# A gated MLP layer on one core: all its input products in one stage with seven-for-eight column pairs, the token mixing moved behind it

## The chip, the cores and the metric

The kernel runs on one core of a Trainium2 chip. What is measured is its time on the device in microseconds (us). The engines are named as in the profile: PE is TensorE's matmul and PEld its weight load, DVE is VectorE, ACT is ScalarE, POOL is GpSimd, and SP starts the weight loads. A line number is one of the kernel's file.

## The reference

One step of a two-layer encoder on two prompt blocks and one sample block of 128 tokens, model width 2048, all in fp32. Layer 0 is attention (two kinds of heads), and the change does not touch it. Layer 1 is a gated MLP of width 4096:

```
u, v, z = rmsnorm(h) @ w_in1                  # three parts, 4096 columns each
vn      = layernorm(v)                        # over all 4096 columns of a token
mixed   = w_sp[g] @ vn + b_sp                 # tokens of a block, causal, per group of 256 columns
h       = h + (u * mixed * silu(z)) @ w_out1
y       = rmsnorm(h)
```

The normalised v of the sample block is an output too. The norm over all columns means that no mixing can start before the whole of v is there.

## The kernel before, in words

Three token blocks (NT = 3, 384 tokens) stand against 16 k-blocks of 128 (KT) and column blocks of 512; u, v and z have eight column blocks each. Every fp32 product is made of three matmuls on halves: each operand is split into a high part and the rest, and hi x hi, hi x lo and lo x hi are added in one PSUM bank (`products`, L94; matmuls L100, L101, L102). A weight unit is one 128x512 block, 256 KB: SP loads it into `raw` (5 buffers), ACT makes `whi` (L84) and DVE `wlo` (L86), 4 buffers each (`wunit`). A dense column block (`dense_nat`, L108) takes three of the four PSUM banks named "d", one for each token block, and runs over the 16 units; hooks given as `between` put other work between its units, with that work's instructions placed behind the splits of the units before. The order on each engine is fixed when the program is built, by a scheduler; each engine takes its own queue in that order.

Before `seven`, layer 1 makes v blocks 0 and 1 densely. Then two column pairs follow, (2,3) and (4,5), in `seven`: for the two prompt blocks and two column blocks, a 2x2 scheme with seven products in place of eight, and four more for the sample block: 11 block products of 24 matmuls where 12 were. It has three phases, `singles`, `chain` and `pair`, each in four steps u over k. In the last two, the operands are sums of weight blocks, made by DVE from loads of 512 KB (`load2`, five buffers named sraw; sums L943) before they are split (shi L90, slo L91; three buffers each); the matmuls are at L930 to L932, into four banks named "a". The blocks v6 and v7 are made the ordinary way between those steps: three units ahead of each step of `chain`, one ahead of each step of `pair`. All v goes to DRAM (`vd`), 768 KB for a block.

Then a loop runs over c = 0..7: z block c, evicted with silu into `gate` (L1139); u block c, multiplied in (L1147); v block c + 1 loaded and normalised meanwhile (L1066, L1067); the mixing of block c, 12 matmuls (L1166 to L1168), the product with the gate (L1170), and the turn: a transposition on DVE (L132) and 16 DMAs on POOL's queue (L135) into gTt, four hi copies on ACT (L1177) and four lo copies on DVE (L1178). After c = 2, 4 and 6 `out1` multiplies 8 more k-blocks by w_out1; the last 8 come behind the loop, the final four of them in a hand-placed stage with the final norm.

Of the kernel before, what the change touches and what calls it, by code (L numbers as in the profile page):

```python
# [15 lines left out]
P = 128  # L16
# [21 lines left out]
def tile_hybrid_step(  # L38
# [828 lines left out]
    with ExitStack() as l1:  # L867
# [6 lines left out]
        vd = [dram.tile([P, NT, 512], F32, name=nm("vd")) for _ in range(8)]  # L874

        with ExitStack() as lv:
            vp = lv.enter_context(tc.tile_pool(name="l1v", bufs=1, reuse_waits="tile"))

            def evict_v(c, o):
                v = slot(F32).rearrange("p (t c) -> p t c", t=NT)  # L880
                for tb in range(NT):
                    S.activation(v[:, tb, :], o[tb], AF.Copy)  # L882
                done_v(c, v)

            def done_v(c, v):
# [28 lines left out]
            def load2(u, half, c):  # L914

                raw = wide()
                nc.sync.dma_start(raw, w_in1[4 * u * P:4 * (u + 1) * P, CW + c * 512:CW + c * 512 + 512].rearrange("(j h p) c -> h p j c", h=2, p=P)[half])
                return raw
# [15 lines left out]
            def seven(c):  # L934

                v0, v1 = (slot(F32).rearrange("p (t c) -> p t c", t=NT) for _ in range(2))
# [8 lines left out]
                def singles(u):  # L945
                    if u == 0:
                        banks("1", "p", "2", "q")
                    b11, b21 = split2(load2(u, 0, c)), split2(load2(u, 1, c))
# [6 lines left out]
                def close_singles():  # L955
                    S.activation(v1[:, 0], m["1"], AF.Copy)
                    S.activation(v1[:, 2], m["p"], AF.Copy)
                    add(v0[:, 0], m["2"], v1[:, 0])
                    add(v0[:, 2], m["q"], v1[:, 2])

                def chain(u):
                    if u == 0:
                        banks("5", "r", "6", "4")
                    b11, b12, b22, b21 = load2(u, 0, c), load2(u, 0, c + 1), load2(u, 1, c + 1), load2(u, 1, c)
# [17 lines left out]
                def pair(u):  # L982
                    if u == 0:
                        banks("3", "s", "7")
                    b22, b12 = load2(u, 1, c + 1), load2(u, 0, c + 1)
# [8 lines left out]
                def close_pair():  # L994
# [4 lines left out]
                    done_v(c, v0)  # L999
                    done_v(c + 1, v1)  # L1000
# [3 lines left out]
            def eight(c):  # L1004
# [3 lines left out]
                def one(k):  # L1008
                    if k == 0:
                        o.extend(dbank() for _ in range(NT))  # L1010
                    ws = [wunit(w_in1[k * P:(k + 1) * P, CW + c * 512:CW + c * 512 + 512], 1, 512)]
                    return lambda: products(o, hh_, hl_, ws, k, range(NT), 0, KT - 1)

                return one, lambda: evict_v(c, o)
# [17 lines left out]
            for c, c8 in ((2, 6), (4, 7)):  # L1032
                (b1, e1), (b2, e2), (b3, e3) = seven(c)
                one, close = eight(c8)
                steps = [(b1, u) for u in range(4)] + [(e1, None)]
                for u in range(4):
                    steps += [(one, 3 * u + i) for i in range(3)] + [(b2, u)]
                steps += [(e2, None)]
                for u in range(4):
                    steps += [(one, 12 + u), (b3, u)]  # L1040
                run(steps + [(e3, None)])
                close()
        for tb in range(NT):
            V.bn_aggr(out=mvr[:, tb, :], in_=stats[:, tb, :, :])
        G.tensor_tensor(out=rsv, in0=mvr[:, :, 1], in1=rstd, op=ALU.mult)
        G.tensor_tensor(out=rsv, in0=rsv, in1=rstd, op=ALU.mult)
        G.tensor_scalar(out=rsv, in0=rsv, scalar1=LN_EPS, scalar2=None, op0=ALU.add)
        G.tensor_tensor(out=rsv, in0=rsv, in1=ex, op=ALU.pow)
        G.tensor_tensor(out=rsv, in0=rsv, in1=rstd, op=ALU.mult)
# [7 lines left out]
        def normalise(c):  # L1057

            cs = slice(c * 512, (c + 1) * 512)
            lg = lp.tile([P, NT * 4, P], F32, tag="gTt", bufs=1, name=nm("lg")).rearrange("p x q -> p (x q)")[:, :1024].rearrange("p (a c) -> p a c", a=2)  # L1060
# [9 lines left out]
        load_v(0)  # L1070
        for _ in normalise(0):
            pass
# [52 lines left out]
        def split_values(c):  # L1125

            vh = lp.tile([P, NT * 4, P], F32R, tag="trn", bufs=1, name=nm("vh")).rearrange("p (t x) q -> p t (x q)", t=NT)
# [5 lines left out]
        vhl = split_values(0)  # L1133
        for c in range(8):
            wTs = [spatial_weights(2 * c + i) for i in range(2)]
            o = dense_nat(w_in1, 0, 2 * CW + c * 512, hh_, hl_)
            gate = lp.tile([P, NT, 512], F32, tag="gate", bufs=1, name=nm("gate"))
            for tb in range(NT):
                S.activation(gate[:, tb, :], o[tb], AF.Silu, scale=rstd[:, tb:tb + 1])  # L1139
            ahead = iter(())  # L1140
            if c < 7:
                load_v(c + 1)
# [3 lines left out]
            for tb in range(NT):  # L1146
                V.scalar_tensor_tensor(out=gate[:, tb, :], in0=o[tb], scalar=rstd[:, tb:tb + 1], in1=gate[:, tb, :], op0=ALU.mult, op1=ALU.mult)  # L1147
            if c == 7:

                for j in range(2):  # L1150
# [8 lines left out]
            for i in range(2):  # L1159
                cs = slice(i * 256, i * 256 + 256)  # L1160
                (wh, wl), (vh, vl) = wTs[i], vhl

                for j, tbs in ((0, slice(0, 2)), (1, slice(2, 3))):
                    n = tbs.stop - tbs.start
# [132 lines left out]
```

## Time and profile before

| | |
|---|---|
| median of 3 runs | 1782.47 us (1780.71 to 1785.07) |
| the profiled execution | 1781.91 us |
| its span | 1779.8 us |
| mean granted TensorE clock | 0.998 |
| PE, DVE, ACT, POOL busy | 1767.2, 1030.3, 740.9, 399.0 us |
| DMA, read and written in HBM | 291.64 MB, 35.71 MB |

The profile is that of one execution. The page gives the busy time of each engine; windows give it for a stretch of time; groups of instructions give count, busy time, mean ns of one, and the idle time ahead of them with what ended it; waits list who waited for whom; a timeline lists instructions with start, length and, in brackets, the idle time before. Matmuls overlap in TensorE's pipeline, so what one costs is the distance of starts, not its own length.

### The profile page before, as it was taken

How to read it: one execution, taken by the hardware profiler on the slowest of the kernel's cores; microseconds unless marked ns; L12 is line 12 of the kernel's file. 1: busy time of each engine (PE TensorE's matmuls, PEld its weight loads, DVE VectorE, ACT ScalarE, POOL GpSimd, SP SyncE). 2: the span in 40 equal slices, each digit the busy share in tenths (PEclk: the TensorE clock that was granted, in tenths of full speed). 3: DMA queues.
4: the chain of work that ended last, by engine and by line, in shares of the span. 5: the costliest groups of instructions: out<-in, count | busy, mean ns of one | idle time of the engine just before them, and what ended most of it. 6: DMA issues, size and time to landing. Idle time of an engine off the chain costs nothing. (4 is left out here: it accounts for less than half of the span.)

```text
span 1779.8 us, 24513 instructions
## 1 busy us (share of the span) xinstructions
PE 1767.2 (99%) x8515; PEld 1464.4 (82%) x8515; DVE 1030.3 (58%) x1674; ACT 740.9 (42%) x1289; POOL 399.0 (22%) x605
## 2 busy tenths in 40 slices
PE   9999999999999999999999999999999999999998
PEld 8978888888888888888887888888888888888887
DVE  6337565457448354677778556555456545454366
ACT  5435354346337244444443433433333333433344
POOL 6525534223311210100112231321021200220020
PEclk9999999999999999999999999999999999999999
DMA  8788989878868977677885655655455643564453
GB/s 228 198 208 202 274 215 229 236 171 217 234 187 213 258 183 165 183 257 229 262 246 185 220 147 158 180 151 154 130 155 156 167 143 125 160 154 135 155 148 119
DMA packets 195244, 335.31 MB, mean 188 GB/s; under 512 B 23768, under 2 KB 62224, under 8 KB 195120
## 3 DMA queue, kind: packets, MB, share of 16 engines
q1 hardware_dynamic: 135888, 242.15, 46.4%
q0 software_dynamic: 28400, 75.47, 17.3%
q10 hardware_dynamic: 30832, 16.13, 3.1%
q8 instruction: 66, 1.08, 0.3%
q14 instruction: 58, 0.48, 0.1%
HBM read 291.64 MB, written 35.71 MB: 184 GB/s over the span
## 5 line engine op out<-in xcount | busy, mean ns | idle before, releaser
L101 PE MATMUL d<-wlo,slot 128*128 128x512 f32 x2157 | 837.8, 389 | 0.0
L102 PE MATMUL d<-whi,slot 128*128 128x512 f32 x2157 | 837.6, 389 | 0.0
L86 DVE TENSOR_TENSOR wlo<-raw,whi 128x512 fp32r<-128x512 f32 x706 | 483.9, 696 | 579.8 <-ACT whi L84 575.9
L84 ACT ACTIVATE whi<-raw 128x512 fp32r<-128x512 f32 x706 | 443.8, 631 | 793.0 <-PE d L102 732.1
L100 PE MATMUL d<-whi,slot 128*128 128x512 f32 x2157 | 761.4, 390 | 1.5 <-ACT whi L84 1.5
L100 PEld LDWEIGHTS d<-whi,slot 128*128 128x128 f32 x2157 | 404.5, 188 | 89.8 <-ACT whi L84 3.1
L101 PEld LDWEIGHTS d<-wlo,slot 128*128 128x128 f32 x2157 | 405.0, 188 | 84.0 <-DVE wlo L86 1.0
L102 PEld LDWEIGHTS d<-whi,slot 128*128 128x128 f32 x2157 | 404.9, 188 | 84.2 <-DVE slot L278 0.3
L135 POOL DMA_DIRECT2D gTt<-trn x128 | 78.1, 617 | 149.2 <-DVE trn L132 110.9
L90 ACT ACTIVATE shi<-sraw 128x1024 fp32r<-128x1024 f32 x56 | 59.4, 1062 | 73.3 <-PE a L932 61.9
L91 DVE TENSOR_TENSOR slo<-sraw,shi 128x1024 fp32r<-128x1024 f32 x56 | 67.7, 1220 | 12.8 <-ACT shi L90 12.7
L464 POOL DMA_DIRECT2D slot<-d x48 | 44.0, 924 | 132.2 <-DMA d<-slot 54.1
L943 DVE TENSOR_TENSOR sraw<-sraw,sraw 128x1024 f32<-128x1024 f32 x32 | 39.1, 1223 | 31.7 <-DMA sraw<-in_w_in_dram 29.8
L1114 POOL DMA_DIRECT2D wr<-in_w_sp_dram x64 | 35.0, 553 | 83.7 <-DVE wT L1118 76.1
L563 POOL DMA_DIRECT2D slot<-wd x32 | 27.1, 855 | 93.9 <-DMA wd<-pr 32.8
L1068 POOL DMA_DIRECT2D out_dram<-v x8 | 4.5, 558 | 183.8 <-DVE v L1067 183.8
L931 PE MATMUL a<-slo,slot 128*128 128x512 f32 x112 | 43.7, 390 | 0.0
L932 PE MATMUL a<-shi,slot 128*128 128x512 f32 x112 | 43.6, 389 | 0.0
L888 POOL DMA_DIRECT2D vd<-slot x8 | 4.4, 551 | 168.6 <-ACT slot L882 162.8
L930 PE MATMUL a<-shi,slot 128*128 128x512 f32 x112 | 41.9, 389 | 0.0
L1107 DVE TENSOR_TENSOR slot<-d,slot 128x512 f32<-128x512 f32 x48 | 31.7, 686 | 11.6 <-PE d L102 11.5
L524 POOL DMA_DIRECT2D kcache<-in_cache_sb_k_dram x32 | 24.9, 786 | 34.0 <-DVE KT L694 34.0
(303 smaller groups left out, 1579.4 us busy)
## 6 DMA issues: line engine op xcount, KB each, us to landing
raw<-in_w_in_dram SPq DMA_DIRECT2D x576, 256.0 KB, 3.3
raw<-in_w_out_dram SPq DMA_DIRECT2D x175, 256.0 KB, 3.5
sraw<-in_w_in_dram SPq DMA_DIRECT2D x64, 512.0 KB, 4.8
slot<-d POOLq DMA_DIRECT2D x48, 192.0 KB, 6.0
d<-slot ACTq DMA_DIRECT2D x24, 256.0 KB, 4.2
vd<-slot POOLq DMA_DIRECT2D x8, 768.0 KB, 7.1
v<-vd POOLq DMA_DIRECT2D x8, 768.0 KB, 6.9
gTt<-trn POOLq DMA_DIRECT2D x128, 48.0 KB, 4.3
```

The source lines that it names most:

```text
L84: highs.append(S.activation(hi, raw, AF.Copy).ins)
L86: splits.append(V.tensor_tensor(out=lo, in0=raw, in1=f32(hi), op=ALU.subtract).ins)
L90: S.activation(hi_out, src, AF.Copy)
L91: V.tensor_tensor(out=lo_out, in0=src, in1=f32(hi_out), op=ALU.subtract)
L100: PE.matmul(o, lhsT=his[k][:, t], rhs=hi[:, 0, :], start=(k == first), stop=False)
L101: PE.matmul(o, lhsT=his[k][:, t], rhs=lo[:, 0, :], start=False, stop=False)
L102: mm = PE.matmul(o, lhsT=los[k][:, t], rhs=hi[:, 0, :], start=False, stop=(k == last))
L135: G.dma_start(dst[32 * j:32 * j + 32, :, 32 * a:32 * a + 32], trn[32 * a:32 * a + 32, :, 32 * j:32 * j + 32])
L464: r = G.dma_start(blk[32 * j:32 * j + 32].rearrange("p h (a d) -> p (h a) d", d=32), d[:, :, 32 * j:32 * j + 32].rearrange("h (a p) d -> p ...
L930: PE.matmul(o, lhsT=xh, rhs=hi[:, j, :], start=(u + j == 0), stop=False)
L931: PE.matmul(o, lhsT=xh, rhs=lo[:, j, :], start=False, stop=False)
L932: PE.matmul(o, lhsT=xl, rhs=hi[:, j, :], start=False, stop=(u == 3 and j == 1))
```

## The change

All column blocks of u, v and z but the last of z and u come into one stage. `seven` takes any two column blocks now. Seven pairs run through it: three of v, (2,3), (4,5), (6,7), and four of z and u, block c of z with block c of u for c = 0..3. Six ordinary blocks, z4, u4, z5, u5, z6, u6, are laid between their steps: three units ahead of each step of `chain`, and one ahead of steps 0 and 2 of `pair`. What is stored is silu(z) * u, into a new DRAM buffer `gd`, 768 KB for a block; statistics of v, silu and the product are done row by row as `seven` closes its banks.

Behind it stand z7 and u7, made densely. The mixing no longer has a loop of its own: `prepare(c)` loads v and the gate of c, makes the spatial weights, normalises, splits, mixes and turns, and yields between these steps. `prepare(0)` and `prepare(1)` are hooked in between the units of z7 and u7, and the others, two each, in the three long `out1` stages. The buffers are regrouped: lg, vh and trn no longer share, the gate has two buffers, and the last weights use what the mixing has left instead of a buffer of their own.

```diff
+            zs = {}
+
+            def evict_z(c, o):
+                zs[c] = nat()
+                for tb in range(NT):
+                    S.activation(zs[c][:, tb, :], o[tb], AF.Silu, scale=rstd[:, tb:tb + 1])
+
+            def gated(z, tb, u):
+                V.scalar_tensor_tensor(out=z[:, tb, :], in0=u, scalar=rstd[:, tb:tb + 1], in1=z[:, tb, :], op0=ALU.mult, op1=ALU.mult)
+
+            def evict_u(c, o):
+                z = zs.pop(c)
+                for tb in range(NT):
+                    gated(z, tb, o[tb])
+                G.dma_start(gd[c], z)
...
-            def seven(c):
-
-                v0, v1 = (slot(F32).rearrange("p (t c) -> p t c", t=NT) for _ in range(2))
+            def seven(a0, a1, row_done, stored):
+
+                v0, v1 = nat(), nat()
...
                     S.activation(v1[:, 2], m["p"], AF.Copy)
                     add(v0[:, 0], m["2"], v1[:, 0])
                     add(v0[:, 2], m["q"], v1[:, 2])
+                    for tb in (0, 2):
+                        row_done(0, v0, v1, tb)
...
-                    done_v(c, v0)
-                    done_v(c + 1, v1)
+                    row_done(0, v0, v1, 1)
+                    for tb in range(NT):
+                        row_done(1, v0, v1, tb)
+                    stored(v0, v1)
...
+            def v_pair(c):
+
+                def row_done(j, v0, v1, tb):
+                    V.bn_stats(out=stats[:, tb, c + j, :], in_=(v0, v1)[j][:, tb, :])
+
+                def stored(v0, v1):
+                    G.dma_start(vd[c], v0)
+                    G.dma_start(vd[c + 1], v1)
+
+                return seven(CW + c * 512, CW + c * 512 + 512, row_done, stored)
+
+            def zu_pair(c):
+
+                def row_done(j, z, u, tb):
+                    if j:
+                        gated(z, tb, u[:, tb, :])
+                    else:
+                        S.activation(z[:, tb, :], z[:, tb, :], AF.Silu, scale=rstd[:, tb:tb + 1])
+
+                return seven(2 * CW + c * 512, c * 512, row_done, lambda z, u: G.dma_start(gd[c], z))
...
-            for c, c8 in ((2, 6), (4, 7)):
-                (b1, e1), (b2, e2), (b3, e3) = seven(c)
-                one, close = eight(c8)
-                steps = [(b1, u) for u in range(4)] + [(e1, None)]
-                for u in range(4):
-                    steps += [(one, 3 * u + i) for i in range(3)] + [(b2, u)]
-                steps += [(e2, None)]
-                for u in range(4):
-                    steps += [(one, 12 + u), (b3, u)]
-                run(steps + [(e3, None)])
-                close()
...
+            NP = 4
+            ordinary = [st for c in range(NP, 7) for st in eight(evict_z, c, 2 * CW + c * 512) + eight(evict_u, c, c * 512)]
...
+            steps = []
+            for make, c in [(v_pair, c) for c in (2, 4, 6)] + [(zu_pair, c) for c in range(NP)]:
...
+                steps += [(part(0), u) for u in range(4)] + [(closing(0), None)]
+                for i, mix in ((1, (3, 3, 3, 3)), (2, (1, 0, 1, 0))):
+                    for u in range(4):
+                        steps += some(mix[u]) + [(part(i), u)]
+                    steps += [(closing(i), None)]
+            run(steps + some(10 ** 6))
...
-        vhl = split_values(0)
-        for c in range(8):
+        def prepare(c):
+
+            load_v(c)
+            gate = lp.tile([P, NT, 512], F32, tag="gate", name=nm("gate"))
+            G.dma_start(gate, gd[c])
             wTs = [spatial_weights(2 * c + i) for i in range(2)]
-            o = dense_nat(w_in1, 0, 2 * CW + c * 512, hh_, hl_)
-            gate = lp.tile([P, NT, 512], F32, tag="gate", bufs=1, name=nm("gate"))
-            for tb in range(NT):
-                S.activation(gate[:, tb, :], o[tb], AF.Silu, scale=rstd[:, tb:tb + 1])
-            ahead = iter(())
...
-                ahead = normalise(c + 1)
-            next(ahead, None)
-            o = dense_nat(w_in1, 0, c * 512, hh_, hl_, between={kp: lambda: next(ahead, None) for kp in (4, 8, 12)})
-            for tb in range(NT):
...
+            yield from normalise(c)
+            yield
+            vh, vl = split_values(c)
+            yield
...
+            yield
             gT = lp.tile([P, NT * 4, P], F32, tag="gTt", bufs=1, name=nm("gTt"))
             turn(gate, gT, lp.tile([P, NT * 4, P], F32, tag="trn", bufs=1, name=nm("trn")))
...
             for k in range(4):
                 h3 = hi[:, k, :].rearrange("p (t q) -> p t q", q=P)
-                turned = S.activation(h3, gk_[:, k], AF.Copy)
+                S.activation(h3, gk_[:, k], AF.Copy)
                 V.tensor_tensor(out=lo[:, k, :].rearrange("p (t q) -> p t q", q=P), in0=gk_[:, k], in1=f32(h3), op=ALU.subtract)
...
-            if c < 7:
-                vhl = split_values(c + 1)
-            if c in (2, 4, 6):
-                out1((c - 2) * 4, 8)
...
+        def both(c):
+            yield from prepare(c)
+            yield
+            yield from prepare(c + 1)
+
+        def hooked(c, n=16):
+            it = both(c)
+            return [lambda: next(it, None) and None for _ in range(n)]
+
+        h = hooked(0)
+        z7 = slot(F32).rearrange("p (t c) -> p t c", t=NT)
+        o = dense_nat(w_in1, 0, 2 * CW + 7 * 512, hh_, hl_, between={kp: h.pop(0) for kp in range(0, KT, 2)})
+        for tb in range(NT):
+            S.activation(z7[:, tb, :], o[tb], AF.Silu, scale=rstd[:, tb:tb + 1])
+        o = dense_nat(w_in1, 0, 7 * 512, hh_, hl_, between={kp: h.pop(0) for kp in range(0, KT, 2)})
+        for tb in range(NT):
+            V.scalar_tensor_tensor(out=z7[:, tb, :], in0=o[tb], scalar=rstd[:, tb:tb + 1], in1=z7[:, tb, :], op0=ALU.mult, op1=ALU.mult)
+        G.dma_start(gd[7], z7)
...
+            out1(k0, 8, hooked(k0 // 4 + 2))
         wl = {}
-        big = lp.tile([P, 18, 512], F32R, tag="wlast", bufs=1, name="wlast")
-        units = [big[:, j, :] for j in range(18)]
-        for _ in range(2):
-            x = lp.tile([P, NT, 512], F32R, tag="v", name=nm("v"))
+        units = []
+        for tag, bufs in (("v", 2), ("v", 2), ("vh", 1), ("vl", 1), ("gate", 2), ("trn", 1), ("gTt", 1)):
+            x = lp.tile([P, NT, 512] if tag in ("v", "vl", "gate") else [P, NT * 4, P], F32R, tag=tag, bufs=bufs, name=nm("wlast"))
+            x = x if tag in ("v", "vl", "gate") else x.rearrange("p x q -> p (x q)").rearrange("p (t c) -> p t c", t=NT)
             units += [x[:, j, :] for j in range(NT)]
...
-        with tc.issue_after(splits[-1]), tc.issue_after(highs[-1]), tc.issue_after(turned.ins):
+        with tc.issue_after(splits[-1]), tc.issue_after(highs[-1]):
```

Two places of the order are shown. In the rows, an arrow goes from the operands to the tile written; numbers tell buffers of one name apart; x4 stands for four alike.

ScalarE, before, at the turn of column 0 (gTt is the turned gate, L1139 is the silu eviction of the next z block, gate_9446 being column 0's):

```order
L84 ACTIVATE whi_10048<-raw_10046 128x512
L84 ACTIVATE whi_10054<-raw_10052 128x512
L1177 ACTIVATE slot_9747<-gTt_9728 128x384 x4
L90 ACTIVATE vh_9757<-v_9450 128x512 x3
L1139 ACTIVATE gate_10034<-d_9791,rstd 128x512
L1139 ACTIVATE gate_10034<-d_9792,rstd 128x512
L84 ACTIVATE whi_10078<-raw_10076 128x512
L1139 ACTIVATE gate_10034<-d_9793,rstd 128x512
```

And now, at the seam between z7 (banks d_12587 to d_12589, evicted at L1239) and u7; the hi copies are those of L1221:

```order
L84 ACTIVATE whi_13002<-raw_13000 128x512
L84 ACTIVATE whi_13008<-raw_13006 128x512
L90 ACTIVATE wTh_12910<-wT_12907 128x256
L90 ACTIVATE wTh_12923<-wT_12920 128x256
L1221 ACTIVATE slot_12857<-gTt_12838 128x384 x4
L1239 ACTIVATE slot_12586<-d_12587,rstd 128x512
L1239 ACTIVATE slot_12586<-d_12588,rstd 128x512
L1239 ACTIVATE slot_12586<-d_12589,rstd 128x512
L84 ACTIVATE whi_13035<-raw_13033 128x512
```

In both, the hi copies stand ahead of a z block's evictions. New is that the block evicted is the one whose last units the mixing itself was hooked between, and that two splits of spatial weights are all that stands between the weight splits and the copies.

TensorE, before, from the last mixing matmul of column 0 (bank a_9723) on; d_9791 is a bank of the next z block:

```order
L1168 MATMUL a_9723<-vh_9169,wTl_9200 128x256
L100 MATMUL d_9791<-whi_9796,slot_6596 128x512
L101 MATMUL d_9791<-wlo_9798,slot_6596 128x512
L102 MATMUL d_9791<-whi_9796,slot_6597 128x512
L100 MATMUL d_9791<-whi_9802,slot_6596 128x512
```

And now, from the last mixing matmul of column 0 (bank a_12803) on; d_12963 to d_12965 are u7's banks, and d_12964 is the bank that z7's d_12587 had:

```order
L1211 MATMUL a_12803<-vh_12750,wTl_12617 128x256
L101 MATMUL d_12963<-wlo_12978,slot_6596 128x512
L102 MATMUL d_12963<-whi_12976,slot_6597 128x512
L100 MATMUL d_12963<-whi_13002,slot_6596 128x512
L101 MATMUL d_12963<-wlo_13004,slot_6596 128x512
L102 MATMUL d_12963<-whi_13002,slot_6597 128x512
L100 MATMUL d_12963<-whi_13008,slot_6596 128x512
L101 MATMUL d_12963<-wlo_13010,slot_6596 128x512
L102 MATMUL d_12963<-whi_13008,slot_6597 128x512
L100 MATMUL d_12964<-whi_12970,slot_6596 128x512
```

The block that follows the mixing runs three banks side by side over two units in the kernel before; now the first bank gets the 12 matmuls of four units by itself, eight of them behind the mixing, before the second bank gets its first.

Over the whole program TensorE's order has 120 rows fewer.

More of the change, by code (lines that the diff above doesn't have):

```diff
@@ L1010, in one @@
                         o.extend(dbank() for _ in range(NT))
[L1011 removed]
+                    ws = [wunit(w_in1[k * P:(k + 1) * P, c0:c0 + 512], 1, 512)]
                     return lambda: products(o, hh_, hl_, ws, k, range(NT), 0, KT - 1)
[L1014 removed]
+                return [(one, k) for k in range(KT)] + [(lambda: evict(c, o), None)]
             def run(steps):
```

108 lines of the change are left out of this document (59 added, 49 removed).

## The prediction

> **What bounds the kernel now.** I read the page's busy times first, then the windows over layer 1 (which begins near 670 us), then TensorE's waits in the chain of waits, and last the timelines where that list named a wait. The page's first part gives each engine's busy time, its share of the span and its instructions.
>
> ```profile
> PE 1767.2 (99%) x8515; PEld 1464.4 (82%) x8515; DVE 1030.3 (58%) x1674; ACT 740.9 (42%) x1289; POOL 399.0 (22%) x605
> ```
>
> TensorE is the bound. The windows say at what pace: start and end, length, then busy time and count of PE, PEld, DVE, ACT and POOL, then the granted clock, the DMA share and GB/s. The rows are the first column pair, the second pair with what follows it, a stretch of the z/u stage, and the end.
>
> ```profile
> 815.00:880.00 65.00, 65.00 (x288) 53.82 (x287) 50.85 (x59) 29.99 (x36) 1.59 (x3) 1.00 0.76 247
> 880.00:980.00 100.00, 98.32 (x432) 80.48 (x431) 76.99 (x94) 41.12 (x49) 20.46 (x36) 1.00 0.73 222
> 1250.00:1400.00 150.00, 150.00 (x666) 124.30 (x665) 78.50 (x121) 54.48 (x90) 26.65 (x45) 1.00 0.51 151
> 1640.00:1780.00 140.00, 131.46 (x614) 110.15 (x612) 76.85 (x136) 53.82 (x104) 14.50 (x24) 0.98 0.47 143
> ```
>
> In the first, 288 matmuls of 128x512 fill 65.00 us with no gap: 65.00 / 288 = 0.2257 us from one start to the next. That is the price of a matmul here, in the pair stage and the plain stage alike; the page's 389 ns each overlap, since they are pipelined. DVE stands at 78% in the first pair, 77% in the second and only 52% in the z/u stretch, so a stage that is pulled from the last kind to the first has much less room beside TensorE. These are all the waits of TensorE that the list of waits has (total us, times, longest):
>
> ```profile
> PE a L931 <- DVE slo L91: 1.7, 1, 1.7
> PE d L100 <- ACT whi L84: 1.5, 3, 0.6
> PE a L226 <- DVE ones L141: 1.1, 1, 1.1
> ```
>
> Layer 1 has one: 1.7 us in the second pair. Before it, hardly anything can be won but by taking matmuls away; afterwards anything that makes TensorE wait is lost in full.
>
> **The change part by part.** The sum is made against the profiled execution, 1781.91 us (span 1779.8 us and 2.1 us around it); the median of the runs is 1782.47 us, 0.6 us above, which I leave out.
>
> *Matmuls taken away.* A column pair costs 11 block products of 24 matmuls for what were 12: 24 fewer for each pair. Two pairs become seven, so 5 x 24 = 120 matmuls go, which is also by how much TensorE's order gets shorter. 120 x 0.2257 = 27.1 us: **-27.1 us**, if TensorE stays as full as it was.
>
> *Seven pair stages for two.* A pair streams its weights about twice, in loads of 512 KB, and splits sums as well. What ended DVE's idle time in the pair stage, then DVE's timeline around the wait of the second pair, then TensorE's, then the same add in the first pair:
>
> ```profile
> DVE sraw L943 <- DMA sraw<-in_w_in_dram: 29.8, 17, 3.6
> ```
>
> ```profile
> 950.05 1.22 DVE L91 TENSOR_TENSOR slo<-sraw,shi 128x1024 fp32r<-128x1024 f32 x1
> ...
> 952.32 0.69 DVE L86 TENSOR_TENSOR wlo<-raw,whi 128x512 fp32r<-128x512 f32 x1
> 956.63 1.23 DVE L943 TENSOR_TENSOR sraw<-sraw,sraw 128x1024 f32<-128x1024 f32 x1 [3.62 <-DMA sraw<-in_w_in_dram]
> 957.77 2.35 DVE L91 TENSOR_TENSOR slo<-sraw,shi 128x1024 fp32r<-128x1024 f32 x2
> ```
>
> ```profile
> 957.00 0.39 PE L930 MATMUL a<-shi,sumh 128*128 128x512 f32 x1
> 959.04 0.50 PE L931 MATMUL a<-slo,sumh 128*128 128x512 f32 x1 [1.66 <-DVE slo L91]
> ```
>
> ```profile
> 861.21 1.23 DVE L943 TENSOR_TENSOR sraw<-sraw,sraw 128x1024 f32<-128x1024 f32 x1 [3.10 <-DMA sraw<-in_w_in_dram]
> ```
>
> Five buffers hold the 512 KB loads. The last load of a pair can start only when the split at 950.05 has released its buffer (951.27); it has landed when the add begins, at 956.63. DVE takes its queue in order, so the splits behind that add wait too, and TensorE, next matmul 2.04 us after the last instead of 0.23, loses 1.8 us there; over the whole window of that pair it is 100 - 432 x 0.2257 = 2.5 us. In the first pair the same add waited 3.10 us and TensorE lost nothing (65.00 of 65.00). So a pair costs between 0 and 2.5 us, and the change gives this phase no further buffer; two ordinary units of weights now lie in it where there were four, but those come behind the point where it pinches. I take the mean of the two pairs seen, 1.25 us: 7 x 1.25 - 2.5 = **+6.3 us**, bounds -2.5 (all clean) and 7 x 2.5 - 2.5 = +15.
>
> *Gates by way of DRAM.* Per column one more store and one more load of 768 KB. The nearest rows are those of v, whose last number is the time to landing:
>
> ```profile
> vd<-slot POOLq DMA_DIRECT2D x8, 768.0 KB, 7.1
> v<-vd POOLq DMA_DIRECT2D x8, 768.0 KB, 6.9
> ```
>
> A gate is asked for a column ahead, that is some 35 us ahead (worked out below) of 6.9 us, and stored pairs earlier. I cost it at nothing; without that cover it would be 6.9 us once, at the first column.
>
> *Mixing beside the last product.* Mixing, turn and splitting of columns 0 and 1 now lie between the units of the last ordinary columns z7 and u7. Here the order speaks, at the place shown above. ScalarE is to make column 0's four hi copies, which need all 16 DMAs of the turn, and only behind them the three evictions of z7. TensorE has one free bank beside z7's three: it does the 12 matmuls of u7's first token block that four weight units allow, eight of them behind the last mixing matmul, and then needs a bank of z7's. In the kernel before, mixing was followed by a column whose three banks had long been evicted. What the turn takes, from the same work for column 1 there: DVE, POOL and ScalarE in the timeline, and the DMAs' time from issue to landing.
>
> ```profile
> 1108.04 0.87 DVE L1170 SCALAR_TENSOR_TENSOR gate<-a,bcol,gate 128x256 f32<-128x256 f32 x2
> 1108.95 1.78 DVE L132 STREAM_TRANSPOSE trn<-gate 128x1536 f32<-128x1536 f32 x1
> ```
>
> ```profile
> 1111.02 6.10 POOL L135 DMA_DIRECT2D gTt<-trn  x10 [18.46 <-DVE trn L132]
> 1117.58 3.65 POOL L135 DMA_DIRECT2D gTt<-trn  x6 [0.46 <-DMA gTt<-trn]
> ```
>
> ```profile
> 1130.22 1.75 ACT L1177 ACTIVATE slot<-gTt 128x384 fp32r<-128x384 f32 x4
> ```
>
> ```profile
> DMA to landing us min/median/max: 2.0/4.3/5.9
> ```
>
> ```profile
> L1139 ACT ACTIVATE gate<-d,rstd 128x512 f32<-128x512 f32 x4 | 2.6, 676 | 0.0
> L91 DVE TENSOR_TENSOR wTl<-wT,wTh 128x256 fp32r<-128x256 f32 x4 | 1.7, 418 | 0.0
> ```
>
> Count from the end of the last mixing matmul, when its gate product can begin (1108.48 in those rows, the second of the two). The transposition ends 2.25 us later (1110.73), the last DMA begins about 12.1 us later (its issue ends at 1121.23, 0.6 us each), and its data land 4.3 us after that, at +16.4. The new order has a spatial weight's split (0.42) ahead of the transposition: +16.9. Then four copies, 1.75, and the first eviction, 0.68: TensorE goes on at +19.3. It ran dry at 8 x 0.2257 = +1.8. That is **+17.5 us**, once, bounds 15 and 20. Landing in 2.0 us instead makes it 15, in 5.9 us with an issue a microsecond slower 20. In the kernel before, these copies came a column's work later: 1130.22 is 9 us after the last issue, and ScalarE had splits to do meanwhile. At the other columns of the new order 11 or 12 weight splits lie between transposition and lo copies, and the next evictions stand ahead of the hi copies, so I price them at nothing.
>
> A gap of such a length is not in the trace; the longest in layer 1 is the 2 us at 957, and the windows show the granted clock at 1.00 there. [...]
>
> *Out-products with two columns' preparation in them.* Groups of a z/u stretch of two columns, with counts, busy time and mean ns:
>
> ```profile
> L86 DVE TENSOR_TENSOR wlo<-raw,whi 128x512 fp32r<-128x512 f32 x56 | 38.1, 690 | 42.0 <-ACT whi L84 42.0
> L1170 DVE SCALAR_TENSOR_TENSOR gate<-a,bcol,gate 128x512 f32<-128x512 f32 (+1 forms) x8 | 4.6, 612 | 0.1
> L1067 DVE SCALAR_TENSOR_TENSOR v<-v,rsv,lg 128x512 f32<-128x512 f32 x6 | 4.5, 751 | 2.0 <-DMA lg<-in_sgu_ln_b_dram 1.9
> L1066 DVE SCALAR_TENSOR_TENSOR v<-v,mvr,lg 128x512 f32<-128x512 f32 x6 | 4.5, 747 | 0.0
> L91 DVE TENSOR_TENSOR vl<-v,vh 128x512 fp32r<-128x512 f32 x6 | 4.0, 686 | 2.3 <-ACT vh L90 2.3
> L132 DVE STREAM_TRANSPOSE trn<-gate 128x1536 f32<-128x1536 f32 x2 | 3.5, 1758 | 0.0
> L1178 DVE TENSOR_TENSOR slot<-gTt,slot 128x384 fp32r<-128x384 f32 x4 | 2.0, 552 | 0.0
> ```
>
> For one column: gate products 2.3, normalising 2.25 + 2.25, vl 2.0, transposition 1.75, four lo copies 4 x 0.552 = 2.2, spatial weights, estimated from the 0.84 of two wTl splits, about 2.9: 15.7 us. An out-product stage has 16 units for each, 16 x 0.69 = 11.0, and 6 additions of about 0.69, 4.1. So 30.8 us of DVE. TensorE has 16 x 9 matmuls and 12 of mixing, 156 x 0.2257 = 35.2 us. DVE goes from 52% to 88%, still under TensorE, and at each mixing point at least 27 matmuls (6.1 us) already split stand in TensorE's order. I take 0, bounds 0 and +6 (one us for each of six columns).
>
> *The rest.* The statistics are taken row by row, and fewer or other buffers serve the last weights: the same instructions off the bound. The tail has the same steps: 0.
>
> Sum: 1781.9 - 27.1 + 6.3 + 17.5 = **1778.6 us**. About 0.3%, 5.3 us, is what a measurement of this kernel can tell from no change; 1777.1 to 1787.8 counts as the same.
>
> **The rivals.** *A, the forecast:* 17.5 us of wait eat most of 27.1: 1778.6. Its own range: 1781.9 - 27.1 - 2.5 + 15 = 1767 to 1781.9 - 27.1 + 15 + 20 = 1790.
>
> *B, the seam costs little:* the turn of column 0 is done by the time z7 ends, because TensorE reaches the mixing later than its place in the order says or the copies are not where the order shows them. For it: the kernel before has no such wait in any of eight columns. Against it: mixing, transposition, copies and evictions stand in that sequence on engines that take their queues in order. 1778.6 - 17.5 = 1761.1 us, faster; with clean pairs too, 1752.3.
>
> *C, slower: the last load of each pair becomes the bound.* It ends on the other side. If TensorE loses in each pair what DVE waited for its load, 3.6 us at most, seven cost 25.2, less the 2.5 there now 22.7: 1781.9 - 27.1 + 17.5 + 22.7 = 1795.0 us. It decides where this term passes 1787.8 - 1772.3 = 15.5 us, that is from (15.5 + 2.5) / 7 = 2.6 us for a pair on. For it: DVE at 77 to 78% there, DMA at 0.73 to 0.76, a 3.1 us wait in both pairs, and gates and their evictions new in four pairs. Against it: one of two pairs hid that wait entirely, and the point is reached with the same matmuls in hand.
>
> *D, the saving is not made:* excluded, as the order is shorter by 120 matmuls of the same kind.
>
> **How the numbers follow.** A 0.6, B 0.2, C 0.2. A's middle lies 1.5 us above the limit of 1777.1, and its ends are 12 us away on either side: 0.23 faster, 0.35 the same, 0.02 slower. B is faster but for 0.01; C is slower but for 0.01. Together: faster by over 0.3% 0.42, within 0.3% 0.37, slower by over 0.3% 0.21. The predicted time is A's, 1778.6 us. The range takes in A (1767 to 1790), goes down to B's 1761 and up to C's 1795, which leaves half of B and half of C out.
>
> **What would show it.** In the profile after: (1) TensorE's count falls by about 120 and full stretches keep 0.2257 us a matmul; a slower pace there would make the first term wrong. (2) In z7/u7 one gap of 15 to 20 us, with the hi copies from the turned gate released by the turn's DMAs and the z7 evictions right behind them; no gap over 5 us there means B. (3) In each of seven pairs at most 2.5 us, with the wait on a slo split behind an add that waited for its load; over 2.6 us in most means C. (4) The out-products without waits on wlo; several us per column there is a cost that I put at 0. (5) The granted clock right after the long gap. Wrong outright would be a wait that recurs per unit or per column.

## The result, and the profile after

The changed kernel takes 1792.55 us in the median of 4 runs (1791.21 to 1793.24), the kernel before 1782.02 beside it: a ratio of 1.0056, with a 95% interval of 1.0038 to 1.0073. The forecast was 1778.6, within 0.3%; it came out slower by 0.6%, inside the range and on the side of rival C. The profiled execution has a span of 1791.5 us, 11.7 above that of before.

The page of the changed kernel, its first part (busy us, share of the span, instructions):

```profile
PE 1748.9 (98%) x8395; PEld 1443.9 (81%) x8395; DVE 1203.1 (67%) x1784; ACT 787.5 (44%) x1273; POOL 407.2 (23%) x621
```

The 120 matmuls are gone (8515 to 8395). What came in their place is in the list of TensorE's waits, changed kernel (us in total, times, longest):

```profile
PE d L100 <- ACT slot L1239: 15.6, 1, 15.6
PE a L946 <- DVE slo L91: 11.5, 12, 2.2
PE a L1209 <- ACT vh L90: 3.5, 2, 1.8
PE a L945 <- DVE slot L958: 2.2, 5, 1.3
```

The first is the seam between z7 and u7, the second and fourth are in the pairs, the third is two mixings in the out-products. First the seam. ScalarE's timeline there, changed kernel:

```profile
1458.09 0.42 ACT L90 ACTIVATE wTh<-wT 128x256 fp32r<-128x256 f32 x1 [5.53 <-DVE wT L1178]
1467.42 1.76 ACT L1221 ACTIVATE slot<-gTt 128x384 fp32r<-128x384 f32 x4 [8.92 <-DMA gTt<-trn]
1469.09 1.82 ACT L1239 ACTIVATE slot<-d,rstd 128x512 f32<-128x512 f32 x3
```

It stands idle for the turn's DMAs with z7's finished banks next in its queue. TensorE's timeline at the same place:

```profile
1452.08 0.28 PE L1211 MATMUL a<-vh,wTl 128*128 128x256 f32 x1
...
1453.79 0.39 PE L102 MATMUL d<-whi,slot 128*128 128x512 f32 x1
1469.81 0.80 PE L100 MATMUL d<-whi,slot 128*128 128x512 f32 x1 [15.63 <-ACT slot L1239]
1470.40 0.63 PE L101 MATMUL d<-wlo,slot 128*128 128x512 f32 x1
1470.83 0.63 PE L102 MATMUL d<-whi,slot 128*128 128x512 f32 x1
```

After its last mixing matmul it did the eight that the prediction counts, stood from 1453.79 to 1469.81, and then went on at 0.43 us a matmul instead of 0.227 for nine steps, until 1473.82. The gap costs 16.02 - 0.23 = 15.8 us and the slow stretch 2.0.

Now the pairs. I call the loss of a stretch what the starts of neighbouring matmuls lie apart beyond 0.2267 us, wherever that is over 0.1 us, summed. Pair by pair that is, in the kernel before, 0 and 2.2 us, and in the changed kernel 0, 1.9, 1.4 (v) and 3.9, 2.6, 6.4, 4.2 (z/u): 20.4 together. The windows of the chain phases alone say where it starts (length, PE's busy time and number of matmuls, clock, DMA share, GB/s). The kernel before:

```profile
810.49:853.33 42.84, 42.84 (x190) 1.00 0.73 230
903.42:946.22 42.80, 42.77 (x189) 1.00 0.75 236
```

And the changed kernel, its first, third, fourth, sixth and seventh pair:

```profile
807.96:850.80 42.84, 42.84 (x191) 1.00 0.73 232
...
991.18:1029.82 38.64, 38.47 (x170) 1.00 0.74 239
1081.42:1121.72 40.30, 38.86 (x169) 1.00 0.72 228
...
1264.88:1306.33 41.45, 39.70 (x172) 1.00 0.70 222
1360.28:1402.52 42.24, 39.74 (x171) 1.00 0.70 224
```

A chain phase held about 190 matmuls before and in the first pair; from the third pair on it holds 170, since a pair brings 14 ordinary units along and not 16: the order draws units forward, and those that the pair phase no longer has are missing in the chain phase. With 170 matmuls, 38.5 us of work, it takes up to 42: TensorE waits for sums and splits there, which it hardly did before (0 and 0.3 us).

By phase the 20.4 us are 10.0 in the chain phases, counted up to the first matmul of the pair phase, 8.5 in the pair phases, which hold 99 matmuls as they did before, and 1.9 in the single products of the second pair, where 105 matmuls stand for 122. What is lost in the pair phases is lost mainly where the kernel before stalled once, behind an add that waits for its load. In the changed kernel's fourth pair, DVE and then TensorE:

```profile
1131.93 1.22 DVE L958 TENSOR_TENSOR sraw<-sraw,sraw 128x1024 f32<-128x1024 f32 x1 [3.43 <-DMA sraw<-in_w_in_dram]
```

```profile
1134.35 0.50 PE L946 MATMUL a<-slo,sumh 128*128 128x512 f32 x1 [1.46 <-DVE slo L91]
```

### The profile page after: what moved, and what is told of

It reads as the page before. It is cut to its first block, busy times and chain, and to the rows that moved or that the text cites. A ratio compares the mean times of both kernels' runs of the same rounds, so it can differ in the third digit from the quotient of the medians.

```text
span 1791.5 us, 24294 instructions
## 1 busy us (share of the span) xinstructions
PE 1748.9 (98%) x8395; PEld 1443.9 (81%) x8395; DVE 1203.1 (67%) x1784; ACT 787.5 (44%) x1273; POOL 407.2 (23%) x621
## 5 line engine op out<-in xcount | busy, mean ns | idle before, releaser
L101 PE MATMUL d<-wlo,slot 128*128 128x512 f32 x1677 | 652.2, 390 | 0.0
L102 PE MATMUL d<-whi,slot 128*128 128x512 f32 x1677 | 650.7, 390 | 0.0
L100 PE MATMUL d<-whi,slot 128*128 128x512 f32 x1677 | 608.4, 391 | 15.6 <-ACT slot L1239 15.6
L86 DVE TENSOR_TENSOR wlo<-raw,whi 128x512 fp32r<-128x512 f32 x546 | 374.7, 696 | 313.0 <-ACT whi L84 311.0
L84 ACT ACTIVATE whi<-raw 128x512 fp32r<-128x512 f32 x546 | 342.3, 630 | 525.9 <-PE d L102 448.1
L100 PEld LDWEIGHTS d<-whi,slot 128*128 128x128 f32 x1677 | 315.3, 188 | 84.1 <-ACT slot L1239 16.1
L102 PEld LDWEIGHTS d<-whi,slot 128*128 128x128 f32 x1677 | 315.3, 188 | 66.0
L90 ACT ACTIVATE shi<-sraw 128x1024 fp32r<-128x1024 f32 x196 | 208.0, 1061 | 272.4 <-PE a L947 228.5
L91 DVE TENSOR_TENSOR slo<-sraw,shi 128x1024 fp32r<-128x1024 f32 x196 | 236.4, 1218 | 36.8 <-ACT shi L90 35.7
L958 DVE TENSOR_TENSOR sraw<-sraw,sraw 128x1024 f32<-128x1024 f32 x112 | 136.9, 1222 | 110.8 <-DMA sraw<-in_w_in_dram 104.0
L946 PE MATMUL a<-slo,slot 128*128 128x512 f32 x392 | 153.2, 391 | 3.3 <-DVE slo L91 3.2
L947 PE MATMUL a<-shi,slot 128*128 128x512 f32 x392 | 152.6, 389 | 0.0
L945 PE MATMUL a<-shi,slot 128*128 128x512 f32 x392 | 147.1, 390 | 0.0
L945 PEld LDWEIGHTS a<-shi,slot 128*128 128x128 f32 x392 | 73.7, 188 | 15.4
L947 PEld LDWEIGHTS a<-shi,slot 128*128 128x128 f32 x392 | 73.7, 188 | 15.2
```

Of the source, the lines that this page charges most:

```text
L84: highs.append(S.activation(hi, raw, AF.Copy).ins)
L86: splits.append(V.tensor_tensor(out=lo, in0=raw, in1=f32(hi), op=ALU.subtract).ins)
L90: S.activation(hi_out, src, AF.Copy)
L91: V.tensor_tensor(out=lo_out, in0=src, in1=f32(hi_out), op=ALU.subtract)
L100: PE.matmul(o, lhsT=his[k][:, t], rhs=hi[:, 0, :], start=(k == first), stop=False)
L101: PE.matmul(o, lhsT=his[k][:, t], rhs=lo[:, 0, :], start=False, stop=False)
```

## The experiments

Where one of them speaks of losses, they are those of the definition above.

**The seam alone.** In column 0 the copies are kept back until z7's evictions are issued; for this they come one hook later, with the first step of column 1's preparation ahead of them:

```diff
+                with ExitStack() as behind:
+                    if c == 0:
+                        behind.enter_context(tc.issue_after(silus[-1]))
+                    S.activation(h3, gk_[:, k], AF.Copy)
```

> The four hi copies of column 0's turned gate are made to stand behind z7's three silu evictions on ScalarE; nothing else is changed. Theory A (the seam: TensorE waited 15.8 us for a bank whose eviction stood behind these copies, and ran 2 us more at the lower clock): the gap goes, no wait of over 3 us takes its place, and the time falls by 16 to 18 us from 1792.5 to about 1775. Rival (the wait only stood in for another one, on DVE's lo copies or the next splits): a gap of 6 to 12 us stays a few matmuls later, and less than 10 us is won.

1780.3 us (10 runs; ratio to before 0.9988, interval 0.9979 to 0.9998): 12.2 us won, where 16 to 18 were expected. The seam's wait is gone from the list of this run, but the mixings' line has grown from 2 waits to 3:

```profile
PE a L946 <- DVE slo L91: 10.6, 10, 2.4
PE a L1209 <- ACT vh L90: 5.3, 3, 1.8
```

The third is that of column 2, and TensorE's timeline shows it dearer than its length:

```profile
1497.25 0.39 PE L102 MATMUL d<-whi,slot 128*128 128x512 f32 x1
1499.44 1.75 PE L1209 MATMUL a<-vh,wTh 128*128 128x512 f32 x4 [1.81 <-ACT vh L90]
1500.99 0.63 PE L1210 MATMUL a<-vl,wTh 128*128 128x512 f32 x1
1501.41 0.63 PE L1211 MATMUL a<-vh,wTl 128*128 128x512 f32 x1
```

Behind 2.0 us of loss the twelve mixing matmuls run at about half the pace, the later ones shown 0.43 us apart, which costs another 1.5 us; the wait at 1573 was followed by such a stretch too, 1.6 us. So the mechanism of the seam is shown, and about 5 of its 17.8 us came back at the mixings behind it.

**More buffers for the loads.**

```diff
-WPITCH = 576
+WPITCH = 544
-                return vp.tile([P, 2, 512], F32, tag="sraw", bufs=5, name=nm("sraw"))
+                return vp.tile([P, 2, 512], F32, tag="sraw", bufs=6, name=nm("sraw"))
-vp.tile([P, 2 * WPITCH], F32R, tag=tag, bufs=3, name=nm(tag))
+vp.tile([P, 1024], F32R, tag=tag, bufs=3, name=nm(tag))
```

> Six buffers for the 512 KB loads instead of five, made room for by smaller padding of the split weights (576 to 544 and 512 columns). Theory L (in the pair stage a load starts only when a split has given its buffer back, so five buffers make the ring that TensorE waits for): the losses of the seven pairs, 20.6 us in the changed kernel, fall under 9, and the time by 11 or more, to 1781 or less. Rival D (DVE's own work, 75 to 80% busy, or the queues' coupling sets the pace): the losses change by less than 4 us and the time stays within 1789 to 1796.

1824.2 us, ratio 1.0239 (1.0218 to 1.026). The pairs lose 21.0 us (0, 2.9, 0, 4.8, 4.5, 6.6, 2.3), so the theory of the five buffers falls as it was put: DVE's waits for loads are nearly what they were, 97.7 us against 104.0. The loss has moved, though: the pair phases lose 1.9 us where they lost 8.5, the chain phases 17.3 where they lost 10.0. As the padding was changed with the buffers, this run can't say why. What made it slower is the padding. In a stretch of the out-products, this run and the changed kernel:

```profile
1500.00:1560.00 60.00, 60.00 (x267) 48.87 (x266) 45.78 (x79) 21.81 (x39) 28.89 (x51) 1.00 0.74 214
```

```profile
1500.00:1560.00 60.00, 60.00 (x272) 49.88 (x271) 51.17 (x86) 24.67 (x45) 26.06 (x46) 1.00 0.80 238
```

Both are full, and in the same time five matmuls fewer are done; a later run has the padding alone.

**Silu at the pair's end.** The two calls of `row_done` move from `close_singles` to `close_pair`.

> In the pairs, the row-by-row work (silu and product, or the statistics) of the first two rows is no longer done when the phase of the single products closes but with the rest at the pair's end. Theory S (ScalarE's silu of the z rows, which waits for DVE's closing sums, holds the splits of the chain phase that stand behind it, and this is why the z/u pairs lose some 4 us each and the v pairs 1): the z/u pairs' losses fall from 16.9 us to 4 to 8, and the time by 8 to 12, to about 1782. Rival L (the loads' ring): the losses stay where they are, within 4 us.

1796.0 us (1789.9 to 1797.3), ratio 1.0071 (1.0052 to 1.0091); losses 0.8, 1.3, 2.4, 3.3, 1.9, 7.0, 4.8, together 21.5. ScalarE's silu is not the cause.

**No z/u pairs.**

```diff
-            NP = 4
+            NP = 0
```

> Only v goes through the seven-product pairs, three of them; z0..z6 and u0..u6 are made as ordinary blocks, the surplus behind the pairs; the rest, seam included, is as in the changed kernel. 96 matmuls more cost 96 x 0.2257 = 21.7 us. Theory Z (four z/u pairs lose 16.9 us between them in the changed kernel, ordinary blocks nothing): 1792.5 + 21.7 - 16.9 = about 1797. If the pairs' losses have nothing to do with the z/u pairs themselves and only move to other places, the time is about 1814.

1790.0 us, ratio 1.0040 (1.0027 to 1.0053). The three v pairs lose 0.1, 1.4 and 2.3. It is 7 us less than the sum of parts gives, and for a reason of another place: the seam's wait is 4.8 us here instead of 15.6. The four z/u pairs of the change saved 21.7 us of matmuls and paid about 17 for it; this run alone cannot say whether they paid as z/u pairs or as late ones. No run shows why the seam's wait shrank.

**By kind or by place.**

```diff
-[(v_pair, c) for c in (2, 4, 6)] + [(zu_pair, c) for c in range(NP)]
+[(zu_pair, c) for c in range(NP)] + [(v_pair, c) for c in (2, 4, 6)]
```

> The four z/u pairs run ahead of the three v pairs; nothing else is changed. Theory C (cover: what a pair loses goes by its place in the stage, since the first two pairs have more ordinary matmuls in their chain phase): the first two pairs lose 2 us or less each though they are z/u pairs, and the later ones, the v pairs among them, 2 to 6 us each; the sum stays at 17 to 24 us and the time within 4 us of 1792.5. Rival Z (by kind): the first four lose 2.5 to 6 us each, the v pairs at the end 0 to 2.

1798.2 us, ratio 1.0099 (1.0081 to 1.0116). Losses: 0.6, 2.4, 1.4, 2.9 in the z/u pairs, 3.1, 4.3, 0.5 in the v pairs. The chain phases of its first pair (z/u) and its fifth and sixth (v):

```profile
812.53:855.37 42.84, 42.84 (x191) 1.00 0.72 226
1178.45:1219.92 41.47, 39.56 (x171) 1.00 0.79 253
1270.76:1311.51 40.75, 38.69 (x168) 1.00 0.76 247
```

A z/u pair with 190 matmuls in its chain phase loses nothing there, and v pairs with 170 lose 2.7 each: rival Z falls. The sum, 15.0, is below the 17 to 24 expected, so place does not give the size of it; the last v pair, at 175, and the third z/u pair, at 168, lost nothing in that phase. The time is 6 us over the changed kernel's all the same: what lies behind the pairs lost 32.2 us instead of 22.2, 18.8 of it the seam's wait.

**More ordinary units to a pair.**

```diff
-            NP = 4
+            NP = 3
-                for i, mix in ((1, (3, 3, 3, 3)), (2, (1, 0, 1, 0))):
+                for i, mix in ((1, (3, 3, 3, 3)), (2, (1, 1, 1, 1))):
```

> Three z/u pairs instead of four, so that z3 and u3 are ordinary blocks too, and 16 ordinary units laid into each of the six pairs instead of 14 (one ahead of every step of the pair phase); the rest, seam included, as in the changed kernel. 24 matmuls more cost 5.4 us. Theory C (cover: with two ordinary units fewer in a pair the chain phase is shorter than its loads, sums and splits take; from the third pair on it has 75 matmuls of ordinary work instead of 93): the six pairs lose 8 us or less together, 20.4 in the changed kernel, and the time is 1792.5 + 5.4 - 12 or more = 1786 or less. Rival Z (z/u pairs lose some 4 us each by what they are): 3 x 4.2 + 3.3 = 16 us lost, 1793.

1779.5 us (10 runs), ratio 0.9992 (0.9982 to 1.0001). The six pairs lose 9.4 us (0.1, 0.8, 3.7, 0, 3.0, 1.9), near the 8 of theory C and far from the 16 of Z. Again the seam's wait is short, 4.9 us, which accounts for the rest of the gain.

**Everything mended.** As above, with four units ahead of each chain step, the seam as in the first experiment, and in columns 2, 4 and 6 one hook more between splitting v and mixing, taken from normalising:

```diff
-                for i, mix in ((1, (3, 3, 3, 3)), (2, (1, 0, 1, 0))):
+                for i, mix in ((1, (4, 4, 4, 4)), (2, (1, 1, 1, 1))):
...
             vh, vl = split_values(c)
             yield
+            if c in (2, 4, 6):
+                yield
```

> Three z/u pairs, 20 ordinary units in each of the six pairs (four ahead of each step of the chain phase, one ahead of each of the pair phase), the silu evictions of z7 ahead of column 0's hi copies, and in columns 2, 4 and 6 the mixing one hook later than the splitting of v. By theory C and the seam: from the 1780.3 us with the evictions ahead, 24 matmuls more +5.4, the pairs' losses from 20 to 4 or less -16, the three mixing waits with their slow stretches, 11 us, to 2 or less -9: about 1761, and under 1782 for certain. Rival (the losses move on: DVE has the same sums and splits to do in less time): 1770 to 1780.

1760.1 us (1758.2 to 1761.6), ratio to the kernel before 0.9879 (0.9863 to 0.9896): it beats both kernels. Its pairs lose 4.4 us (0, 1.5, 0, 0, 2.9, 0), and this is its list of TensorE's waits:

```profile
PE a L226 <- DVE ones L141: 1.1, 1, 1.1
PE d L100 <- DVE slot L897: 0.9, 2, 0.6
PE a L946 <- DVE slo L91: 0.9, 2, 0.5
```

The window over its out-products has no gap, with DVE at 151.36 of 190 us, 80%:

```profile
1450.00:1640.00 190.00, 190.00 (x856) 157.82 (x856) 151.36 (x257) 76.13 (x136) 88.45 (x153) 1.00 0.78 226
```

**The waits mended, the pairs left.** The same without the change of pairs and units (NP = 4, 14 units).

> The changed kernel with its seven pairs and 14 units in each as they are; only the waits behind them are mended: z7's silu evictions ahead of column 0's hi copies, and in columns 2, 4 and 6 the mixing one hook later. If the parts add up (seam 15.8 + 2.0 of slow clock, mixing waits 2 x 2.3, both gone; the pairs' losses of 20 us stay): 1792.5 - 22.4 = 1770, which against the 1760.1 of three z/u pairs with 20 units makes the cover worth 20 - 4.4 - 5.4 = 10 us. Rival (the kernel with three pairs was fast because of the mended waits alone): 1754 to 1760, since it has 24 matmuls fewer.

1775.9 us (1773.1 to 1776.9), ratio 0.9971 (0.9959 to 0.9984). The pairs lose 16.9 us (0, 1.3, 3.4, 2.9, 3.2, 2.9, 3.3), what lies behind them 2.6. The parts add up to within 6 us, and the rival's 1754 to 1760 falls. The run with three pairs and 20 units is 15.8 us faster: its pairs lose 12.5 us less, for 24 matmuls, 5.4 us, more. So by the losses the cover is worth about 7 us net, not the 10 expected; 2.6 us more are those behind the pairs, and the rest was not broken down.

**The same units laid otherwise.** Here only the units are moved, 16 to each of six pairs and none left for the seventh:

```diff
-                for i, mix in ((1, (3, 3, 3, 3)), (2, (1, 0, 1, 0))):
+                for i, mix in ((1, (3, 3, 3, 3)), (2, (1, 1, 1, 1))):
```

> As the run with seven pairs and the waits mended (1775.9 us), but the same 96 ordinary units are laid 16 to each of the first six pairs, which leaves the seventh none. Matmuls, pairs and their order stay the same. Theory C (cover): pairs three to six, which lost 2.9 to 3.4 us each with 14 units, lose 0 to 1.7 each, 6 us or more less together; the seventh pair has only its own 264 matmuls, 60 us, for sums, splits and loads that took DVE some 70 us busy in 90, and loses 6 us or more alone. Rival Z (what a pair loses does not hang on its ordinary units): pairs three to six stay at 2.5 to 3.5 and the seventh too.

1790.8 us, ratio 1.0069 (1.0051 to 1.0086). Pairs three to six lose 3.0, 0.3, 2.7 and 1.9, together 7.9 where it was 12.4: less by 4.5, not by 6. (In the other three runs with 14 units and this order of pairs the same four lost 12.8 to 14.5.) The seventh loses 4.7, not over 6, for it was not bare: the order drew z7's own units into it, 157 matmuls in its chain phase. So the direction is C's and the size less than expected. The time tells nothing of the pairs, since the order behind them shifted too and TensorE waited 13.6 us for hi copies.

**The padding alone,** in the kernel before:

```diff
-WPITCH = 576
+WPITCH = 544
```

> The kernel before with one number changed: the split weights' buffers are 544 columns apart instead of 576 (the 512 used are the same). In the run with six load buffers, which had this too, matmuls on these buffers started 0.2318 us apart instead of 0.2270 and the time was 1824. Theory P (the distance of the buffers that TensorE reads, while ScalarE and VectorE write the next ones, sets the pace of its matmuls): 0.2318 us here too, some 7900 matmuls by 0.0048, +38 us, 1815 to 1822. Rival (the slower pace belonged to the sixth buffer or its loads): 1782, within 3 us.

1812.3 us, ratio 1.0175 (1.0159 to 1.019). Its row for the stretch that the prediction quotes with 666 matmuls:

```profile
1250.00:1400.00 150.00, 150.00 (x651) 121.56 (x650) 76.14 (x120) 53.50 (x90) 18.01 (x31) 1.00 0.48 145
```

By the distances of their starts in layer 1, matmuls on the split weights lie 0.2317 us apart here and 0.2268 in the kernel before; on the pairs' own buffers, which are spaced by the same number, 0.2274 and 0.2269. In this stretch the clock is granted in full, and TensorE waits for nothing. The one number is the cause. How it acts was not tried: by the distance itself or by where the buffers come to lie, by the writes beside the reads or by the reads alone.

## Why the prediction was wrong

**Matmuls taken away, -27.1 us: right.** 120 fewer, and full stretches keep their pace: 0.2267 us from start to start in both kernels. The 0.2257 of the prediction comes from a window's count, which takes in matmuls that overlap its ends; on 120 that makes 0.1 us.

**The seam, +17.5 us: right.** 15.8 us, 17.8 with the slow stretch. The chain ran as it was counted, 1.8 us faster: the copies began 15.1 us after the end of the last mixing matmul, not 16.9, and TensorE went on at +17.5, not +19.3, for the last of the turn's DMAs landed 2.0 us after its issue, not 4.3. The granted clock right after the gap was 0.50, until 1474.0; that is the slow stretch, 2.0 us, for which the sum has no term. A wait of 2.15 us was followed by the lower clock too, as the last section shows.

**The seven pairs, +6.3 us: the step that failed.** It is +18.2 (20.4 less the 2.2 of before), beyond the bound of +15. The place that was priced came out as priced: 7 x 1.25 = 8.75 us were put on the pair phases, and they lost 8.5, 1.5 of it by the lower clock. The failing words are that two of four ordinary units less "come behind the point where it pinches". I took the place where the second pair had stalled for the only narrow one, and put the other phases at nothing: they lost 11.9 us, 10.0 of it in the chain phases. For units are not bound to the step that they are written ahead of: the order draws them forward, and those missing from the pair phase are missing in the chain phase, 170 matmuls for 190. There, 42.8 us had covered four loads, three sums and three splits a step, and 38.5 mostly do not. What is lost goes with the cover: 2.9 us a pair with 14 units (2.1 to 3.1 in the other runs with seven such pairs), 1.6 with 16, 0.7 with 20 (20.4 / 7, 9.4 / 6, 4.4 / 6), at the same sums and the same loads. It does so in the mean and not in every pair: from the third pair on, 25 chain phases with 167 to 173 matmuls, from the five runs that have seven such pairs and the wide padding, lost 0 to 4.1 us, 1.75 in the mean, and the eight with 182 to 189, from the two runs that lay 16 units to a pair, 0 to 2.4, 0.85 in the mean. The row to see it in was there: DVE at 77 to 78% in a stage whose own matmuls fill only 264 x 0.2257 = 60 of 93 us.

**Rival C** had the right sign, a price of 3.6 us a pair and a turning point of 2.6; measured were 2.9, and 1792.5 us for its 1795.0. That it came so near is in part luck: at the place that it names, the last load of a pair, 1.2 us a pair were lost, under its turning point, and the rest in phases that it left out. There too, five of the six late splits that cost the chain phases most stood behind an add that had waited for its load, 1.4 to 2.3 us; but a sixth buffer for the loads did not lower the sum. I gave it 0.2 because one pair had hidden that wait. In the changed kernel the first two pairs, whose chain phases still hold some 190 matmuls, hide it in their pair phases as well, and the other five do not.

**Out-products, 0: wrong by 4.4 us,** within its bound of 6. DVE, at 85% in the stretch of 1500 to 1560 shown above, did not stop TensorE, as was said; but the two mixings waited for v's high halves, which ScalarE's queue has behind weight splits that themselves wait for TensorE (the one at 1581.84 had waited 0.95 us):

```profile
1581.42 0.39 PE L102 MATMUL d<-whi,slot 128*128 128x512 f32 x1
1583.56 1.25 PE L1209 MATMUL a<-vh,wTh 128*128 128x512 f32 x4 [1.76 <-ACT vh L90]
```

**Gates by way of DRAM, 0: right** as far as can be seen; no wait of TensorE names them.

The sum with the measured sizes, -27.1 + 17.8 + 18.2 + 4.4 = +13.3, stands to the 11.7 us between the spans; smaller losses ahead of the pairs (1.8 us for 4.1) take 2.3 off it, which leaves 0.7 unexplained.

That the cover counts is shown by moving units alone (12.4 to 7.9 us in four pairs); open stays what exactly sets the pace in the chain phase. It is not the silu or the kind of pair, and more load buffers alone did not mend it. The three buffers of split sums, which ScalarE waits for on TensorE (228.5 us over the seven pairs), would be the next to try; no run had a fourth.

## What to carry to other kernels

Where a stage of heavy preparation is covered by other work laid between, the cover is a term of the sum like any other: count it per phase, in the order as it is built and not as it is written, before spending some of it on more such stages. An engine that evicts finished banks must not have a wait for a slow transfer ahead of the eviction in its queue; here four copies in the wrong place cost two thirds of what 120 matmuls had saved. And TensorE was busy for 99% of the span before: of the 17.8 + 18.2 + 4.4 = 40.4 us that the new waits and slow stretches cost here nearly all went into the time, so a change that removes its work must be checked for waits, place by place, before its matmuls are counted as a gain.

## What the runs showed of the hardware

In the changed kernel's sixth pair a wait of 2.15 us was followed by the lower clock:

```profile
1316.98 0.39 PE L945 MATMUL a<-shi,sumh 128*128 128x512 f32 x1
1319.52 0.50 PE L946 MATMUL a<-slo,sumh 128*128 128x512 f32 x1 [2.15 <-DVE slo L91]
...
1320.67 0.63 PE L947 MATMUL a<-shi,suml 128*128 128x512 f32 x1
1321.10 0.63 PE L945 MATMUL a<-shi,slot 128*128 128x512 f32 x1
```

Seven matmuls start 0.43 us apart, 1.4 us more. The granted clock in three windows there that follow one another (length, PE's busy time and number of matmuls, clock, DMA share, GB/s):

```profile
1316.99:1320.40 3.41, 1.26 (x6) 1.00 0.03 13
1320.40:1323.81 3.41, 3.41 (x10) 0.50 0.90 271
1323.81:1327.22 3.41, 3.41 (x17) 1.00 0.95 304
```

Before its last 5.5 us the changed kernel's trace has two stretches at half clock: this one, 3.41 us long, and that of the seam, 17.07 us from 1456.94 on, five times as long; they begin 136.53 us apart, 40 times 3.41. Cut into pieces of 3.41 us from there, without the first 12 us and the last 4 us of its matmuls, the trace has 511 pieces at full clock. TensorE stood idle for 2.4 and 2.9 us in the two that were followed by half clock, and for 1.9 at most in the other 509. In the kernel before, cut in the same way from its one stretch at half clock (the last 8.9 us, where TensorE has no matmuls), it was 1.6 at most in 514 pieces, and none was followed by half clock. (Idle is counted here from 0.227 us after a start to the next one, in proportion less for narrower matmuls.) The wait of 1.81 us at 1499 in the first experiment was followed by matmuls 0.43 us apart; that of 1.76 us at 1583 in the changed kernel, 1.6 us of it in one piece, was not: the clock stayed at 1.00, and the loss at 1.9 us. No run was made to try what decides it. With the losses of these three, 2.0 + 1.5, 2.3 + 1.4 and 1.9 us, my estimate for a wait of 2 us in this kernel is 2 to 4.

And the number that spaces the buffers of split weights changed the pace of this kernel's matmuls: 544 columns of four bytes instead of 576, with the same 512 used, cost 0.0049 us of each matmul on them (0.2317 for 0.2268), 31 us of the kernel before (1812.3 for 1781.1).
